# Token-major gates of the "b" heads on GpSimd, and attention units split and turned in pairs

## The chip, the cores and the metric

One core of one Trainium2 chip. The metric is the device time of one execution in microseconds (us). The engines are called PE (TensorE, matrix products), DVE (VectorE), ACT (ScalarE), POOL (GpSimd) and SP (SyncE, which here only issues DMAs).

## The reference

One encoder layer over 1024 tokens of width 1024, in float32. Two groups of attention heads run side by side; each has a gate; their gated outputs are projected, added to the input and normalised.

```python
h = x @ w_in                                   # columns: q_a k_a v_a z_a q_b k_b v_b z_b
y_a = neighborhood_attention(q_a, k_a, v_a, rel_bias)   # 8 heads of 64; grid 16 x 64,
                                                        # window 8 rows x 16 columns, 2-D bias
y_b = windowed_gqa_with_sink(rotary(q_b), rotary(k_b), v_b, sink)  # 8 query heads, 2 kv heads,
                                                        # |i - j| <= 128, one sink logit a head
mixed = concat(y_a * silu(z_a), y_b * silu(z_b))
x = layer_norm(alpha * x + mixed @ w_out, ln_gain, ln_bias)
```

## The kernel before, in words

float32 operands are kept as two float16 parts, a high and a low one, each scaled by a power of two. A product takes three matmuls: high x high, high x low, low x high.

**Stages.** First x and the weights of V are loaded and split, and V is computed. Then come 21 projections of 128 columns each, in the order of the list `ORDER`: `zb0..3` and `z0..3` are the gates of the "b" and "a" heads (two heads in each), `kb`, `qb0..3`, `k0..3`, `q0..3` the keys and queries. The first six (`NPRO`) run by themselves, in the prologue. The other 15 are "fill": their matmuls are spread among the attention's steps by a table of due steps (`FILL_AT`), so that PE always has something to do. At the end the output projection (L1031) and the normalisation follow.

**A projection** (`project`, L379) puts 128 output features on the partitions and 512 tokens in the free dimension. For each half of the tokens it runs 8 blocks of the inner dimension times 3 products, 24 matmuls, each with the weights stationary and 512 tokens moving. Gates are evacuated as SiLU (L338, or L341 and L342).

**Attention** runs over 128 units: 64 of the "b" heads (4 pairs of heads p, 2 heads j, 8 blocks of 128 queries) and then 64 of the "a" heads (p, j, 4 column bands, 2 row halves). Four units in a row are a quad. The loop over steps i emits, for several units in different stages:

- `stage_qk(u)` at step u: two score matmuls (L816, L817) into a PSUM bank of tag "s" (4 banks in turn), and one DVE instruction (L826) that adds mask or bias and takes the row maximum;
- `stage_exp(u)` at the end of step u: the exponential on ACT (L842), written back into the same PSUM bank, with the row sum;
- `stage_tr(u)` at step u+1: the high part by an ACT copy (L852), the low part by a DVE instruction (L853), both into an SBUF tile `split` (6 in turn), and a transposing DMA on SP (L856) into a tile `tr` (9 in turn);
- `stage_pv(q)` nine steps after a quad's first unit: attention times V on PE (L881) for the quad's four units;
- `stage_on(q)` one step later: DVE multiplies by the reciprocal row sums (L887, L890) into the tile `on`, with tokens on the partitions;
- `stage_ot(q)` for the second head of each pair: four PE transposes (L901) turn `on` to features on partitions, and DVE multiplies it into the gate (L904 for "b", L910 for "a").

Inside the loop the program order is kept on every engine (`manual_schedule`), and each engine runs its instructions in that order. Other work (splitting weights, evacuating projections, loading W_out) waits in a queue for each engine; `pop` takes an operation or two from a queue at fixed places of a step: for ACT after `stage_tr` (urgent ones) and after `stage_exp`, for DVE before `stage_exp`.

**The operand of the output projection** is the gated output, split in a high part (ACT, L1013) and a low part (POOL, L1014), by `m_queue` at the steps in `M_AT` for the "b" heads and in the last stage for the "a" heads.

Of the kernel before, what the change touches and what calls it, by code (L numbers as in the profile page):

```python
# [15 lines left out]
S = 1024  # L16
# [11 lines left out]
LTT, LPP, BP, BH, BR, ND, NA, NX, F1 = 1, 6, 2, 9, 5, 1, 1, 6, 0.2  # L28
NSPLIT, NP = 6, 2
ORDER = ["zb0", "z0", "zb1", "kb", "qb0", "z1", "qb1", "zb2", "qb2", "k0", "qb3", "zb3", "q0", "k1", "q1",  # L30
# [6 lines left out]
ZTAG = {"z3": "zv", "zb3": "zc", "z2": "zs", "zb1": "zd", "zb2": "ze"}  # L37
# [10 lines left out]
M_AT = [105, 112, 118, 120]  # L48
# [13 lines left out]
def hybrid_block(ctx, tc, xT, x, wt, wv, wo, bias, sink, gain, lbias, cos, sin, bmask, out):  # L62
# [9 lines left out]
    ps1 = ctx.enter_context(tc.tile_pool(name="ps1", bufs=1, space=PS))  # L72

    def bank(tag):
        bufs = {"pj": 2, "s": 4, "t": 2}[tag]
        return (ps1 if bufs == 1 else ps2).tile([128, 512], F32, tag=tag, name=f"ps_{tag}", bufs=bufs)
# [270 lines left out]
    def z_col(e):  # L347
        i = 0 if e in (4, 0, 5) else 1 if e == 1 else 2
        return zc[:, i:i + 1]
# [7 lines left out]

    def project(name):
        n = ORDER.index(name)
# [45 lines left out]
    with ExitStack() as vctx:  # L405
# [162 lines left out]
        banks = [bank(t) for t in tags]  # L568
# [49 lines left out]
        part = {i: bank(tags[i]) for i in (0, 1, 2, 3, 6, 7)}  # L618
# [138 lines left out]
    split = [ap.tile([128, 3, 2, 128], F16, name=f"split{i}", bufs=1) for i in range(NSPLIT)]  # L757
# [36 lines left out]
    def stage_qk(u):  # L794
        g, p, j, t, _ = u
        n, _c = geom(u)
        ps = bank("s")
# [31 lines left out]
        st[u, "ps"] = ps  # L829
        st[u, "nm"] = nm  # L830

    def stage_exp(u):
        n, _c = geom(u)
        m = n + 1 if u[0] == "b" else n
        sn, nm = st.pop((u, "sn")), st.pop((u, "nm"))
        pt = st.pop((u, "ps"))
        k = units.index(u) % 4
        if k == 0:
            st["sm"] = ap.tile([128, 4], F32, tag="sm", name="sm", bufs=4)
        sm = st["sm"]  # L840
        st[units.index(u) // 4, "sm"] = sm
        nc.scalar.activation(pt[:, :m], sn[:, :m], AF.Exp, bias=nm, scale=-1.0, accum_out=sm[:, k:k + 1])  # L842
        st[u, "p"] = pt

    def stage_tr(u):
        g, p, j, t, _ = u
        n, ch = geom(u)
        pt = st.pop((u, "p"))
        c, m = ch[0], len(ch)
        hl = split[units.index(u) % NSPLIT]  # L850
        src = pt[:, :n].rearrange("p (k c) -> p k c", c=c)
        nc.scalar.activation(hl[:, :m, 0, :c], src, AF.Copy, scale=PSCALE)  # L852
        nc.vector.scalar_tensor_tensor(hl[:, :m, 1, :c], src, PSCALE, hl[:, :m, 0, :c],  # L853
                                       op0=ALU.mult, op1=ALU.subtract)
        tr = ap.tile([128, 6, 128], F16, tag="tr", name="tr", bufs=BH)
        nc.sync.dma_start(tr[:, :2 * m, :], hl[:, :m].rearrange("p k i c -> p (k i c)"), transpose=True)  # L856
        st[u, "tr"] = tr
# [24 lines left out]

    def stage_on(q):
# [4 lines left out]
        if j == 0:  # L888
            on[g, p, h] = ap.tile([128, 4, 2, HD], F32, tag="on", name="on", bufs=2)
        nc.vector.tensor_mul(on[g, p, h][:, :, j, :], ps[:, :4 * HD].rearrange("p (m e) -> p m e", e=HD),  # L890
                             ri.unsqueeze(2).to_broadcast([128, 4, HD]))

    def stage_ot(q):
        g, p, j, h = quad(q)
        if j == 0:
            return
        need(*stk_ops.get(f"zb{p}" if g == "b" else f"z{p}", ()))
# [4 lines left out]
        if g == "b":  # L902
            z = zt[4 + p][:, 512 * h:512 * h + 512]
            nc.vector.scalar_tensor_tensor(z, ps, z_col(4 + p), z, op0=ALU.mult, op1=ALU.mult)  # L904
        else:
            for i in range(2):
                b = 2 * h + i
                z = zt[p].rearrange("p (r c) -> p r c", c=GW)[:, :, 16 * b:16 * b + 16]
                src = ps[:, 256 * i:256 * i + 256].rearrange("p (r c) -> p r c", c=16)
                nc.vector.scalar_tensor_tensor(z, src, z_col(p), z, op0=ALU.mult, op1=ALU.mult)  # L910
# [19 lines left out]
    def m_alloc(e):  # L930
        if e >= 4:
            t = big_tile(f"m{e}", (128, 2, S), F16)
        else:
            t = tiles["fp"].tile([128, 2, S], F16, tag="m", name=f"m{e}", bufs=4)
        mh[e], ml[e] = t[:, 0, :], t[:, 1, :]

    def m_split(e, sl, hi, lo):
        hi(mh[e][:, sl], zt[e][:, sl])
        lo(ml[e][:, sl], zt[e][:, sl], mh[e][:, sl])  # L939
# [69 lines left out]
    def m_queue(e):  # L1009
        m_alloc(e)  # L1010
        m_ops[e] = []
        for h in (slice(0, 512), slice(512, S)):
            o = enq("act", lambda h=h: nc.scalar.copy(mh[e][:, h], zt[e][:, h]))  # L1013
            m_ops[e].append(enq("pool", lambda h=h: nc.gpsimd.tensor_sub(  # L1014
                ml[e][:, h], zt[e][:, h], mh[e][:, h]), o))
# [5 lines left out]
    def out_mms(t, a, ps, es, c=(0, 512)):  # L1021
        o, w = c
        ts, cs = slice(128 * t, 128 * t + 128), slice(o, o + w)
        ps = ps[:, o:o + w]
        for e in es:
# [4 lines left out]
            for i, (lh, rh) in enumerate(((mh[e], woh), (mh[e], wol), (ml[e], woh))):  # L1030
                nc.tensor.matmul(ps, lh[:, ts], rh[:, cs],  # L1031
# [16 lines left out]
    def final():  # L1048
# [7 lines left out]
        for e in EO[4:]:  # L1056
            m_split(e, slice(0, 512), nc.scalar.copy, nc.vector.tensor_sub)
            for n in (WO_SEQ.index((e, 0)), WO_SEQ.index((e, 1))):
                wo_split(n)
        for e in EO[4:]:  # L1060
            m_split(e, slice(512, S), nc.scalar.copy, nc.vector.tensor_sub)
        gb, bb = gain_tile[0], zslot("bb")
# [113 lines left out]
    def gain_load():  # L1176
        gain_tile.append(zslot("gb"))
# [3 lines left out]
    for i in range(-LD, NU + LO):  # L1181
# [25 lines left out]
        if i == 131:  # L1207
            enq("sp", gain_load, *m_ops[4])
# [22 lines left out]
        if 0 <= i - LT < NU:  # L1231
            stage_tr(units[i - LT])
# [8 lines left out]
        pop("dve", ND if i < M_AT[1] else 2, same=True)  # L1241
        if i < NU:
            stage_exp(units[i])
        pop("act", NA if i < M_AT[0] and len(queues["act"]) < 5 else 2)
# [80 lines left out]
```

## Time and profile before

| | |
|---|---|
| median of 3 runs | 445.71 us (445.67 to 446.71) |
| the profiled execution | 446.49 us, span 444.7 us |
| busy share of the span | PE 98%, DVE 77%, ACT 69%, POOL 50% |
| granted TensorE clock, mean | 0.995 |
| attention of the "b" units | 121.8 to 237.5 us after the span's start |
| attention of the "a" units | 237.5 to 355.1 us |

In rows of the timeline the first two numbers are an instruction's start and its duration in us; then come engine, line, operation, output <- inputs, partitions x elements, and how many were merged. In rows of groups the numbers behind the bar are busy us and mean ns of one, and behind a second bar the idle us before them with what ended it. In rows of waits they are the total, the number of times, and the longest. Matmuls overlap, so their price is read from one start to the next and not from the durations.

### The profile page before, as it was taken

Reading aid. Unit: us, or ns where it says so; the run is one execution under the profiler, and the core shown is the slowest. Engines: PE = TensorE matmul, PEld = TensorE weight load, DVE = VectorE, ACT = ScalarE, POOL = GpSimd, SP = SyncE. Lnnn points to the kernel's source line nnn. Section 1 sums busy time; section 2 is a strip of 40 time slices with the busy share of each in tenths; the row PEclk is TensorE's granted clock in tenths of the full one; section 3 lists DMA queues with packets and bytes.
Section 4 is the critical chain, followed back from the end, with each engine's and each line's share of the span. In section 5 each row is a group of like instructions: output and inputs, shape, how many; then the busy total and the mean of one; then the engine's idle time right before and its main releaser. Section 6 shows DMA issues by size and latency. Waiting matters only on the chain.

```text
span 444.7 us, 9505 instructions
## 1 busy us (share of the span) xinstructions
PE 437.5 (98%) x3289; PEld 255.5 (57%) x3289; DVE 344.2 (77%) x849; ACT 308.3 (69%) x700; POOL 221.6 (50%) x235
## 2 busy tenths in 40 slices
PE   9999999999999999999999999999999999999994
PEld 8997754444445565655565655656555654444453
DVE  5978967438986898887988888888878837589944
ACT  5759789766499988887868887888778946302401
POOL 0110074646839558866506767765574405205740
PEclk9999999999999999999999999999999999999997
DMA  8921469984659999587978899998999998103612
GB/s 272 390 91 60 145 235 339 336 292 169 213 127 214 206 190 181 98 162 143 164 127 175 169 182 180 213 170 213 192 204 253 167 172 347 55 0 102 232 69 72
DMA packets 133841, 81.39 MB, mean 183 GB/s; under 512 B 101280, under 2 KB 113440, under 8 KB 133536
## 3 DMA queue, kind: packets, MB, share of 16 engines
q1 hardware_dynamic: 133648, 80.64, 75.4%
q8 instruction: 26, 0.43, 0.4%
q14 instruction: 23, 0.19, 0.2%
q10 hardware_dynamic: 144, 0.13, 0.1%
HBM read 50.34 MB, written 9.96 MB: 136 GB/s over the span
## 4 chain that ended last, share of the span: by engine, by line
PE 91%; DMA 3%; POOL 3%; DVE 1%; issue 1%; ACT 1%; SPq 0%; POOLq 0%; DVEq 0%; ACTq 0%
PE ps_pj L379 44%; PE ps_s L1031 9%; PE ps_s L486 6%; PE ps_t L881 6%; PE ps_pj L1031 5%; PE ps_t L1031 5%; PE ps_s L816 4%; PE ps_s L817 4%; PE ps_pj L486 3%; PE ps_t L486 3%; DMA bias<-in_bias 3%; PE ps_t L901 1%; POOL wl L205 1%; PE ps_t L412 1%; POOL ks L295 1%
## 5 line engine op out<-in xcount | busy, mean ns | idle before, releaser
L379 PE MATMUL ps_pj<-xf,wh 128*128 128x512 f16 x672 | 202.1, 379 | 0.1
L379 PE MATMUL ps_pj<-xf,wl 128*128 128x512 f16 x336 | 127.3, 379 | 0.0
L379 PEld LDWEIGHTS <-wh 128*128 128x128 f16 x672 | 63.7, 98 | 60.4 <-DVE ks L263 0.5
L842 ACT ACTIVATE ps_s<-sn,nm 128x385 f32<-128x385 f32 (+3 forms) x128 | 70.1, 548 | 25.1 <-DVE nm L826 24.6
L853 DVE SCALAR_TENSOR_TENSOR split<-ps_s,split 128x384 f16<-128x384 f32 (+2 forms) x128 | 65.7, 513 | 27.5 <-ACT split L852 25.9
L1031 PEld LDWEIGHTS <-m 128*128 128x128 f16 x432 | 40.0, 98 | 41.1 <-DVE m L939 0.2
L852 ACT ACTIVATE split<-ps_s 128x384 f16<-128x384 f32 (+2 forms) x128 | 57.8, 452 | 2.5 <-DMA tr<-split 0.2
L204 POOL TENSOR_SCALAR wr<-wr,wsc 128x512 f32<-128x512 f32 x26 | 20.6, 791 | 68.1 <-ACT wh L199 61.6
L379 PEld LDWEIGHTS <-wl 128*128 128x128 f16 x336 | 32.9, 98 | 37.4
L826 DVE CUSTOM_DVE_ANT_0 sn<-ps_s,bm,nsk 128x384 f32<-128x384 f32 (+1 forms) x64 | 40.7, 636 | 2.0 <-PE ps_s L817 1.7
L1031 PE MATMUL ps_s<-wo,m 128*128 128x512 f16 (+1 forms) x192 | 40.8, 366 | 0.0
L816 PE MATMUL ps_s<-ks,qs 128*128 128x384 f16 (+4 forms) x128 | 39.2, 306 | 0.3 <-DVE qs L263 0.3
L817 PE MATMUL ps_s<-ks,qs 128*128 128x384 f16 (+4 forms) x128 | 39.2, 306 | 0.0
L826 DVE CUSTOM_DVE_ANT_0 sn<-ps_s,bias,sg 128x264 f32<-128x264 f32 (+1 forms) x64 | 35.0, 547 | 4.5 <-issue 1.5
L881 PEld LDWEIGHTS <-tr 128*128 128x128 f16 (+1 forms) x1104 | 36.6, 98 | 2.2
L205 POOL TENSOR_TENSOR wl<-wr,wh 128x512 f16<-128x512 f32 x26 | 32.7, 1257 | 2.2
L788 POOL TENSOR_SCALAR bias<-bias,rsg 128x552 f32<-128x552 f32 (+1 forms) x24 | 19.1, 797 | 23.8 <-DMA bias<-in_bias 22.6
L295 POOL COPY ks<-ks 64x512 f16<-64x512 f16 x40 | 26.0, 661 | 7.1 <-DVE ks L263 2.8
L1086 ACT ACTIVATE sd<-mv,eps 128x1 f32<-128x1 f32 x8 | 2.4, 295 | 36.5 <-DVE mv L1084 35.2
L1031 PE MATMUL ps_pj<-wo,m 128*128 128x512 f16 (+1 forms) x144 | 26.2, 326 | 0.0
L1130 POOL TENSOR_TENSOR xr<-xr,gb 128x512 f32<-128x512 f32 x7 | 9.8, 1396 | 32.4 <-ACT xr L1127 32.4
L842 ACT ACTIVATION_READ_ACCUMULATOR ps_s<-sn,nm 128x1 f32 x128 | 24.4, 190 | 0.0
(188 smaller groups left out, 813.8 us busy)
## 6 DMA issues: line engine op xcount, KB each, us to landing
ws<-in_wt SPq DMA_DIRECT2D x15, 512.0 KB, 5.9
wr<-in_wt SPq DMA_DIRECT2D x26, 256.0 KB, 3.6
wor<-in_wo SPq DMA_DIRECT2D x22, 256.0 KB, 3.5
bias<-in_bias SPq DMA_DIRECT2D x16, 276.0 KB, 3.3
xr<-in_x SPq DMA_DIRECT2D x8, 512.0 KB, 9.6
out<-xr SPq DMA_DIRECT2D x15, 256.0 KB, 2.1
bias<-in_bias SPq DMA_DIRECT2D x8, 368.0 KB, 3.8
wvraw<-in_wv SPq DMA_DIRECT2D x9, 320.0 KB, 5.8
```

Source lines behind the costliest of these rows:

```text
L205: nc.gpsimd.tensor_sub(l, raw, h)
L295: nc.gpsimd.tensor_copy(t[o, sl], t[a, sl])
L379: nc.tensor.matmul(ps, a[:, k % 4, :], mv, start=(k == 0 and i == 0), stop=(k == KT - 1 and i == 2))
L486: nc.tensor.matmul(ps[:, :320], lh[:, ts], rh[:, cs], start=(k == ko[0] and i == 0), stop=(k == ko[-1] and i == 2))
L816: nc.tensor.matmul(ps[:, :m], q, sl[0], start=True, stop=False)
L817: nc.tensor.matmul(ps[:, :m], q, sl[1], start=False, stop=True)
L826: nc.vector.tensor_tensor_reduce(sn[:, :m], ps[:, :m], bias_t, sg[:, c:c + 1], init, op0=ALU.add, op1=ALU.min, accum_out=nm)
L842: nc.scalar.activation(pt[:, :m], sn[:, :m], AF.Exp, bias=nm, scale=-1.0, accum_out=sm[:, k:k + 1])
L852: nc.scalar.activation(hl[:, :m, 0, :c], src, AF.Copy, scale=PSCALE)
L853: nc.vector.scalar_tensor_tensor(hl[:, :m, 1, :c], src, PSCALE, hl[:, :m, 0, :c], op0=ALU.mult, op1=ALU.subtract)
L881: nc.tensor.matmul(ps[:, HD * m:HD * m + HD], a, b_, start=(i == 0), stop=(i == len(mms) - 1))
L1031: nc.tensor.matmul(ps, lh[:, ts], rh[:, cs], start=(e == EO[0] and i == 0), stop=(e == EO[-1] and i == 2))
```

## The change

1. **Gates of the "b" heads by tokens.** The `zb` projections get a routine of their own, `project_rows`, with the tokens on the partitions: x is stationary, 128 tokens at a time, and 128 weight columns are moving. A half is 4 token blocks x 8 x 3 = 96 matmuls of 128 columns into the same bank. All four `zb` are now in the prologue; `z0` and `z1` take the places of `zb2` and `zb3` in the fill.
2. **The product with the gate.** `stage_on` of a "b" quad scales while it normalises and queues a GpSimd multiplication of `on` into the gate (16 of 128x256 in all). `stage_ot` does nothing for "b".
3. **Turning the product.** `m_queue` splits the gated output as before (ACT, POOL) into a tile `hr`, and two transposing DMAs a head pair then write the parts, features on the partitions, over the gate's own tile. `M_AT` moves these steps from 105..120 to 26..80.
4. **Attention units in pairs.** PSUM tag "s" is now two tiles of two banks. Units 2k and 2k+1 share one. `stage_tr` runs every second step, at step 2k+2, with one ACT copy, one DVE instruction and one transposing DMA for both units (two copies and two DVE instructions where the sizes differ, as in the first and the last pair of eight "b" units). There are 3 `split` tiles and 4 `tr` tiles of twice the size.
5. Gain and bias of the normalisation get tiles of the large pool instead of gate slots.

```diff
-ORDER = ["zb0", "z0", "zb1", "kb", "qb0", "z1", "qb1", "zb2", "qb2", "k0", "qb3", "zb3", "q0", "k1", "q1",
+ORDER = ["zb0", "zb1", "zb2", "kb", "qb0", "zb3", "qb1", "z0", "qb2", "k0", "qb3", "z1", "q0", "k1", "q1",
-M_AT = [105, 112, 118, 120]
+M_AT = [26, 42, 57, 80]
...
+    def pair_bank():
+        return ps2.tile([128, 2, 512], F32, tag="s", name="ps_s", bufs=2)
...
+    def project_rows(name):
+        n = ORDER.index(name)
+        w_split(2 * n + 2)
+        for half in range(2):
+            ps = new_group()
+            need(w_ops[2 * n], w_ops[2 * n + 1])
+            for c in range(96):
+                t, k, i = c // 24, c // 3 % 8, c % 3
...
+                ts = slice(128 * t, 128 * t + 128)
+                h, l = parts[2 * n + k // 4]
+                a, b = ((x16h, h), (x16l, h), (x16h, l))[i]
+                nc.tensor.matmul(ps[:, ts], a[half, k][:, ts], b[:, k % 4, :], start=(c % 24 == 0), stop=(c % 24 == 23))
+                if c % 4 == 3 and c < 95:
+                    yield
+            groups.append(evac(name, half, ps))
+            yield
...
     def stage_qk(u):
-        ps = bank("s")
+        if units.index(u) % 2 == 0:
+            halves_s.clear()
+            st["pair"] = pair_bank()
+        ps = st["pair"][:, units.index(u) % 2, :]
...
+    def stage_tr(k):
+        pt = st.pop((k, "pair"))
+        two = [units[2 * k], units[2 * k + 1]]
+        hl = split[k % NSPLIT]
+        tr = ap.tile([128, 12, 128], F16, tag="tr", name="tr", bufs=BH)
...
+        for src, dst, f in parts_:
+            h, l = (dst[:, :, :, 0, :], dst[:, :, :, 1, :]) if f is not None else (dst[:, :, 0, :], dst[:, :, 1, :])
+            nc.scalar.activation(h, src, AF.Copy, scale=PSCALE)
+            nc.vector.scalar_tensor_tensor(l, src, PSCALE, h, op0=ALU.mult, op1=ALU.subtract)
+        w = 2 * (len(sizes[0][1]) + len(sizes[1][1]))
+        nc.sync.dma_start(tr[:, :w, :], hl.rearrange("p k i c -> p (k i c)")[:, :128 * w], transpose=True)
...
     def stage_on(q):
+        nc.vector.scalar_tensor_tensor(o, src, z_col(4 + p), rb, op0=ALU.mult, op1=ALU.mult)
+        z = zt[4 + p].rearrange("p (t j e) -> p t j e", j=2, e=HD)[:, 4 * h:4 * h + 4, j, :]
+        gate_ops.setdefault(4 + p, []).append(enq("pool", lambda: nc.gpsimd.tensor_mul(z, z, o), prio=0.6))
...
     def m_queue(e):
+            o = enq("act", lambda hr=hr, z=z: nc.scalar.copy(hr[:, :, 0, :], z), *gate_ops[e])
+            o = enq("pool", lambda hr=hr, z=z: nc.gpsimd.tensor_sub(hr[:, :, 1, :], z, hr[:, :, 0, :]), o)
+            m_ops[e].append(enq("sp", lambda hr=hr, out16=out16: nc.sync.dma_start(
+                out16, hr.rearrange("p t i f -> p (t i f)"), transpose=True), o))
...
-        if 0 <= i - LT < NU:
-            stage_tr(units[i - LT])
+        if 0 <= i - LT < NU and (i - LT) % 2 == 1:
+            stage_tr((i - LT) // 2)
```

131 lines of the change are left out of this document (77 added, 54 removed).

## The prediction

> **What bounds the kernel now.** I read the page first: the span, the busy shares, and the chain of work that ended last.
>
> ```profile
> span 444.7 us, 9505 instructions
> PE 437.5 (98%) x3289; PEld 255.5 (57%) x3289; DVE 344.2 (77%) x849; ACT 308.3 (69%) x700; POOL 221.6 (50%) x235
> PE 91%; DMA 3%; POOL 3%; DVE 1%; issue 1%; ACT 1%; SPq 0%; POOLq 0%; DVEq 0%; ACTq 0%
> ```
>
> TensorE (PE) is busy 98% and is 91% of the chain. "Busy" alone proves little, so next I read PE's own waits:
>
> ```profile
> PE ps_t L1111 <- ACT dr L1109: 1.8, 1, 1.8
> PE ps_t L412 <- DVE warm L127: 1.0, 1, 1.0
> PE ps_s L816 <- DVE qs L263: 0.3, 1, 0.3
> ```
>
> That is all: 3.1 us, and only 0.3 us of it between the first projection and the tail. So PE is never held up, and two things move the time: PE work added or taken away, at full price, and anything that makes PE wait where today it waits for nobody. The profiled execution took 446.49 us around a span of 444.7; that is 0.78 above the median of 445.71. I add the sum to the profiled one and take the 0.78 off at the end.
>
> **PE's own work.** The prices come from starts in the timeline, because matmul durations overlap:
>
> ```profile
> 157.17 0.60 PE L901 MATMUL ps_t<-identf,on 128*128 128x128 f32 x4
> 157.61 1.13 PE L881 MATMUL ps_t<-vb,tr 128*128 128x64 f16 x33
> 158.57 0.60 PE L379 MATMUL ps_pj<-xf,wh 128*128 128x512 f16 x2
> 159.00 0.38 PE L379 MATMUL ps_pj<-xf,wl 128*128 128x512 f16 x1
> 159.22 0.59 PE L379 MATMUL ps_pj<-xf,wh 128*128 128x512 f16 x2
> ...
> 434.08 2.84 PE L1031 MATMUL ps_pj<-wo,m 128*128 128x128 f16 x48
> 436.76 0.65 PE L1104 MATMUL ps_t<-bb,identf 128*128 128x256 f32 x2
> ```
>
> Three 512-column matmuls go in 159.22 - 158.57 = 0.65 us, 216.7 ns each. Forty-eight 128-column ones, each with its own weight load, go in 2.68 us: 55.8 ns each. The four "zb" projections have 4 x 2 x 24 = 192 of the first kind (41.6 us); by tokens they become 4 x 2 x 96 = 768 of the second (42.9 us): **+1.3 us**. Could the four times as many weight loads show? The 33 attention-times-V matmuls load new weights every 0.96/33 = 29 ns, so a load hides behind 55.8 ns.
>
> The transposes of the "b" heads go: eight times four, and four take 157.61 - 157.17 = 0.44 us, so **-3.5 us**.
>
> The first projection now asks for both halves of its weights almost at once:
>
> ```profile
> 59.27 1.16 POOL L205 TENSOR_TENSOR wl<-wr,wh 128x512 f16<-128x512 f32 x1
> 59.37 0.59 PE L379 MATMUL ps_pj<-xf,wh 128*128 128x512 f16 x2
> ```
>
> It starts at 59.37. In token order the second half's low part is needed after 14 matmuls, 14 x 0.056 = 0.8 us later, at 60.15; GpSimd finishes it at 60.43: **+0.3 us**. In the old order it was needed 14 x 0.217 = 3 us in, and hidden. PE's own sum is -1.9 us. If nothing else happened, the time would be 443.8.
>
> **What the pairs do to PSUM.** Today each unit has one of four banks, and bank i is needed again by unit i+4, three steps after the step that empties it. After the change the banks come as two pairs. A pair is emptied by one ScalarE copy (high part) and one VectorE subtraction (low part) in the step of unit 2k+2; the scores of unit 2k+4, two steps later, need it back. PE takes its instructions in order, so when that wait is not met everything behind it stands: fill matmuls, scores, attention times V.
>
> Does it matter? Look at how the two engines hand the work to each other, one quad (two pairs) of the "b" heads; of the rows between, those of the even units are left out:
>
> ```profile
> 152.18 0.67 DVE L826 CUSTOM_DVE_ANT_0 sn<-ps_s,bm,nsk 128x384 f32<-128x384 f32 x1
> ...
> 153.12 0.59 ACT L842 ACTIVATE ps_s<-sn,nm 128x385 f32<-128x385 f32 x1
> 153.72 0.72 ACT L199 ACTIVATE wh<-wr,wsc 128x512 f16<-128x512 f32 x1
> 154.33 0.48 ACT L852 ACTIVATE split<-ps_s 128x384 f16<-128x384 f32 x1
> 154.85 0.56 DVE L853 SCALAR_TENSOR_TENSOR split<-ps_s,split 128x384 f16<-128x384 f32 x1 [0.30 <-ACT split L852]
> 155.32 0.17 DVE L887 RECIPROCAL ri<-sm 128x4 f32<-128x4 f32 x1
> 155.52 0.42 DVE L890 TENSOR_TENSOR on<-ps_t,ri 128x256 f32<-128x256 f32 x1
> 155.87 0.67 DVE L826 CUSTOM_DVE_ANT_0 sn<-ps_s,bm,nsk 128x384 f32<-128x384 f32 x1
> 156.58 0.59 ACT L842 ACTIVATE ps_s<-sn,nm 128x385 f32<-128x385 f32 x1 [0.18 <-DVE nm L826]
> 157.19 0.71 ACT L199 ACTIVATE wh<-wr,wsc 128x512 f16<-128x512 f32 x1
> 157.81 0.47 ACT L852 ACTIVATE split<-ps_s 128x384 f16<-128x384 f32 x1
> 158.31 0.56 DVE L853 SCALAR_TENSOR_TENSOR split<-ps_s,split 128x384 f16<-128x384 f32 x1
> 158.78 0.67 DVE L826 CUSTOM_DVE_ANT_0 sn<-ps_s,bm,nsk 128x384 f32<-128x384 f32 x1
> ```
>
> This is the loop of the odd units: bias and maximum (L826), exponential (L842), whatever ScalarE has queued (L199 here), copy (L852), subtraction (L853), whatever VectorE has queued (L887, L890), and only then the L826 of the unit two further. Both engines run in program order, so it is a true loop. It took 158.78 - 152.18 = 6.60 us for two pairs, of which 0.23 is ScalarE coming late at 153.12 (0.94 us after L826 started, against 0.71 at 155.87 to 156.58). Bare: 6.37.
>
> In the changed order the same instructions stand in this loop, but the copy and the subtraction now carry both units, while the even unit's share has left the place where it ran beside the loop. What 384 more columns cost comes from the small and the large form (the large ones are in the fence above: 0.48 and 0.56):
>
> ```profile
> L852 ACT ACTIVATE split<-ps_s 128x256 f16<-128x256 f32 x15 | 5.7, 381 | 0.4
> L853 DVE SCALAR_TENSOR_TENSOR split<-ps_s,split 128x256 f16<-128x256 f32 x15 | 6.3, 422 | 2.6 <-ACT split L852 2.4
> ```
>
> ScalarE: (480 - 381)/128 = 0.77 ns a column, +0.30 us; VectorE: (560 - 422)/128 = 1.08 ns, +0.41. So +0.71 a pair, and this quad's loop becomes 6.37 + 1.42 = 7.8 us. PE's pace:
>
> ```profile
> L816 PE MATMUL ps_s<-ks,qs x64: 269/326/326, 121.8 to 236.2; 128*128 128x384 f16 x48, 128*128 128x256 f16 x16
> L816 PE MATMUL ps_s<-ks,qs x64: 276/304/326, 237.5 to 355.1; 128*128 128x264 f16 x16, 128*128 128x288 f16 x16, 128*128 128x352 f16 x16, 128*128 128x384 f16 x16
> ```
>
> "b": (237.5 - 121.8)/32 = 3.62 us a pair, less 3.5/32 for the transposes, 3.51. "a": (355.1 - 237.5)/31.5 = 3.73. Two "b" pairs are 7.0 us of PE against 7.8 of the loop: the saving in instructions on ScalarE and VectorE is real, but the loop gets longer, and overtakes PE.
>
> To see whether that quad is typical I added up the same pieces (without VectorE's waits for PE) at 31 odd "b" units and 30 odd "a" units; the first and last of each:
>
> ```profile
> 127.24 0.67 DVE L826 CUSTOM_DVE_ANT_0 sn<-ps_s,bm,nsk 128x384 f32<-128x384 f32 x1
> 239.21 0.53 DVE L826 CUSTOM_DVE_ANT_0 sn<-ps_s,bm,nsk 128x256 f32<-128x256 f32 x1
> 242.74 0.51 DVE L826 CUSTOM_DVE_ANT_0 sn<-ps_s,bias,sg 128x288 f32<-128x288 f32 x1
> 350.68 0.61 DVE L826 CUSTOM_DVE_ANT_0 sn<-ps_s,bias,sg 128x384 f32<-128x384 f32 x1
> ```
>
> "b": 3.35 us a pair now. Half the pairs join units of unequal size (the first two and last two blocks); these keep two copies and two subtractions, which overlap, and add only 0.4 to 0.5, so the mean becomes 3.96. "a": 3.23 now, sizes 288 and 384 in turn, becomes 3.86. The excess over PE is 0.45 x 32 = 14.4 us in "b" and 0.13 x 32 = 4.2 in "a". Single pairs run from 2.5 to 6.7 us, so how much is paid depends on PE's lead: a running sum over the 61 pairs gives 16 us with a lead of 2 us and 24 with 1 us. The lead is about 3 x 1.8 steps less the bare loop's 3.5, some 1.8. I take **+18 us**.
>
> **What else moves.** Groups of instructions, the time from issue to landing of the transposes, and one stretch of the tail:
>
> ```profile
> L904 DVE SCALAR_TENSOR_TENSOR z<-ps_t,zc,z 128x512 f32<-128x512 f32 x8 | 6.0, 747 | 0.0
> L1099 POOL TENSOR_TENSOR xr<-xr,gb 128x256 f32<-128x256 f32 x1 | 0.7, 728 | 0.2 <-DVE stats L1080 0.2
> DMA to landing us min/median/max: 2.5/3.4/6.2
> 440.00:442.00 2.00, 0.69 (x2) 0.00 (x0) 0.56 (x1) 0.37 (x1) 0.00 (x0) 0.50 0.23 71
> ```
>
> L904 leaves VectorE (8 x 0.75 = 6 us), but it ran in odd steps, outside the loop: no gain. Its product becomes 16 GpSimd multiplications of 256 columns, 16 x 0.73 = 12 us on an engine at 50%: off the path, because the first reader of the gated "b" heads is the output projection after step 121, some 50 steps later; without that cover it would be those 12 us. The eight 512-column copies of L1013 move forward out of the late "a" units; one that lands between exponential and copy lengthens the loop as L199 does above (153.72 to 154.33), by 0.6, so 0 to 5 us together; I take 0, because half the slots are beside the loop and the queue gives one copy a step, and keep 5 for the range. Scaling inside L890 is one more scalar in the same pass: 0. On SP, 64 larger transposing DMAs replace 128, and eight more are queued; whoever is behind them on SP waits at most for their issue, and attention times V comes five steps after the last transpose. Gain and bias of the norm load earlier, which removes waits in the tail that PE does not feel: 0.
>
> **Sum.** 446.49 + 1.3 + 0.3 - 3.5 + 18 = 462.6 in a profiled execution; less 0.78, **461.8 us**. Its own range: 453 if ScalarE's queued work shifts to the even slots (0.15 less a pair in "b") and "a" stays hidden; 472 with a lead of 1 us and the L1013 copies in the loop.
>
> **Rivals.** (1) *The loop does not bind* (chance 0.20, faster): PE's lead covers it, because the 6 us of L904 and the shorter totals let VectorE catch up, or the halves of a pair come free separately. The point is a loop mean under 3.51. For it: the loop today, 3.35, never stops PE; against it, today's loop leaves so little that +0.4 is enough. Time: 443.8. (2) *The doubled transposes land late* (0.05, slower): the median is 3.4, the slowest 6.2. A pair's transpose has about three steps, 5.5 us, before PE reads it once PE waits for banks; twice the data at twice 3.4 would miss by 1.3 us in 32 quads, some of it inside waits already there: about 475. (3) *The clock drops* (0.03): the last row in the fence above is no term of the sum but shows the granted clock (its third number from the end): 0.50 in two us near the end, in which PE has little to do. If the waits gather in a few pairs, such as those with a loop of 6.7 us, PE pauses 3 us and may come back at half speed; doubling the 3.5 us of PE work of three such pairs adds 10 us: 472. Against it: the mean wait is 0.3 us a pair. [...] (4) *The gains and waits cancel* (0.03): within 0.3% of before, which is about what a measurement of this kernel can tell.
>
> **Chances and range.** The forecast has 0.69; with rivals 2 and 3, slower is 0.77; same 0.03; faster 0.20. As both signs count, the range reaches from rival 1 to the forecast's upper end: 443.5 to 473; the forecast's own is 453 to 472.
>
> **What would show it.** In the profile after: PE's waits list L816 behind VectorE's subtraction or "split" with 10 to 25 us in all, PE busy falls to about 94%, the score matmuls of "b" take 3.9 to 4.0 us a pair instead of 3.62. The prologue is 1.6 us longer, the final projection unchanged, and the L853 of equal pairs take 0.95 us. If PE's waits stay under 2 us, the loop argument is wrong and rival 1 holds; if they name the transposes at L881, rival 2.

## The result, and the profile after

The changed kernel takes **513.96 us** (median of 6 runs, 511.74 to 514.91) against 445.91 for the kernel before (445.67 to 446.71) on the same chip: a ratio of 1.152, 95% interval 1.1495 to 1.1545. The forecast was 461.8 with a range to 473. The sign was right; the size was wrong by 52 us.

The page of the changed kernel, first the busy shares and the chain, then PE in 40 slices:

```profile
span 512.5 us, 10275 instructions
PE 448.9 (88%) x3833; PEld 277.4 (54%) x3833; DVE 340.7 (66%) x793; ACT 306.0 (60%) x652; POOL 233.0 (45%) x248
PE   9999999998767878886877789899997979999995
PE 21%; issue 7%; ACT 6%; DVE 6%; DMA 3%; POOL 3%; SPq 1%; POOLq 0%; DVEq 0%; ACTq 0%
```

PE falls from 98% to 88% busy, and the holes lie in the slices of attention (122.9 to 422.6 us) and in the last slice, which was as empty before. No other engine has become the bound: VectorE and ScalarE were 77% and 69% busy and are now 66% and 60%. Everybody waits for somebody.

PE's score matmuls, and what ended the idle time in front of them (total us, number of times); below that, who else waits most:

```profile
L856 PE MATMUL ps_s<-ks,qs x128: 269/322/406, 122.9 to 422.6; 128*128 128x384 f16 x64, 128*128 128x256 f16 x16, 128*128 128x264 f16 x16, 128*128 128x288 f16 x16
  ACT ps_s L883: 40.9, 45
  DVE sn L861: 7.5, 5
  DVE split L907: 3.3, 3
```

```profile
ACT ps_s L883 <- DVE nm L866: 74.4, 71, 3.8
```

The forecast had PE waiting for the subtraction (L907 now, L853 before): the profile puts 3.3 us down to it. What PE waits for is the **exponential** (L883, 40.9 us), which in the kernel before held up no score matmul at all. All of the 53.5 us idle in front of the scores stands before scores of *odd* units, none before even ones. The stops that the profile puts down to another engine are the same stop: the odd scores start 0.04 to 0.06 us after the last row of the even unit's exponential there too, as here, where it ends at 208.50 + 0.19 = 208.69 us and a subtraction happens to end with it:

```profile
208.50 0.19 ACT L883 ACTIVATION_READ_ACCUMULATOR ps_s<-sn,nm 128x1 f32 x1
208.74 0.32 PE L856 MATMUL ps_s<-ks,qs 128*128 128x384 f16 x1 [0.94 <-DVE split L907]
```

So nearly the whole 53.5 us is the exponential's.

One pair in the timeline of the changed kernel (start, duration, engine, line; in brackets the idle time before and what ended it). Rows of other lines are left out:

```profile
152.42 0.57 ACT L883 ACTIVATE ps_s<-sn,nm 128x385 f32<-128x385 f32 x1
152.92 0.18 ACT L883 ACTIVATION_READ_ACCUMULATOR ps_s<-sn,nm 128x1 f32 x1
...
153.16 0.32 PE L856 MATMUL ps_s<-ks,qs 128*128 128x384 f16 x1 [1.66 <-ACT ps_s L883]
153.79 0.68 DVE L866 CUSTOM_DVE_ANT_0 sn<-ps_s,bm,nsk 128x384 f32<-128x384 f32 x1 [0.30 <-ACT z L350]
...
154.51 0.59 ACT L883 ACTIVATE ps_s<-sn,nm 128x385 f32<-128x385 f32 x1 [0.83 <-DVE nm L866]
155.03 0.19 ACT L883 ACTIVATION_READ_ACCUMULATOR ps_s<-sn,nm 128x1 f32 x1
156.93 0.62 ACT L268 CAST qs<-rp_raw 64x512 f16<-64x512 f32 x1 [1.71 <-POOL rp_raw L324]
157.46 0.80 ACT L906 ACTIVATE split<-ps_s 128x768 f16<-128x768 f32 x1
158.16 0.57 ACT L883 ACTIVATE ps_s<-sn,nm 128x385 f32<-128x385 f32 x1
...
158.90 0.27 PE L856 MATMUL ps_s<-ks,qs 128*128 128x256 f16 x1 [1.60 <-ACT ps_s L883]
```

Read it as a ring. The even unit's exponential ends at 153.10, and 0.06 us later the odd unit's scores start, after 1.66 us of idle PE. The two touch different banks: the exponential writes columns 0 to 384 of the pair's tile, the scores write from column 512 on. Nothing in the arithmetic asks for this order, but the program has it: both halves are now one tile, and the odd unit's first score matmul waits until the exponential in that tile is done. (That the joint tile is the reason is an inference here; the runs below test it.) So the ring closes: even exponential (152.42) to odd scores (153.16), to the odd bias and maximum (153.79), to the odd exponential (154.51, until 155.22), to the copy of this pair (0.70 us, 157.46 to 158.16), and to the even exponential of the next pair, which stands behind it in ScalarE's order. Without the gap from 155.22 to 157.46 that is 0.74 + 0.63 + 0.72 + 0.71 + 0.70 = 3.50 us a pair, and PE itself needs 3.51 (as the prediction worked out). That leaves no slack; whatever else ScalarE has in its queue between the odd exponential and the copy goes on top. Here that is a cast which itself waited 1.71 us for GpSimd, and the pair took 158.16 - 152.42 = 5.74 us.

### The profile page after: what moved, and what is told of

Read it like the earlier page. It is cut to its first block, busy times and chain, and to the rows that moved or that the text cites. A ratio compares the mean times of both kernels' runs of the same rounds, so it can differ in the third digit from the quotient of the medians.

```text
span 512.5 us, 10275 instructions
## 1 busy us (share of the span) xinstructions
PE 448.9 (88%) x3833; PEld 277.4 (54%) x3833; DVE 340.7 (66%) x793; ACT 306.0 (60%) x652; POOL 233.0 (45%) x248
## 5 line engine op out<-in xcount | busy, mean ns | idle before, releaser
L416 PE MATMUL ps_pj<-xf,wh 128*128 128x512 f16 x544 | 165.7, 383 | 0.0
L883 ACT ACTIVATE ps_s<-sn,nm 128x385 f32<-128x385 f32 (+3 forms) x128 | 70.2, 548 | 75.0 <-DVE nm L866 74.4
L416 PE MATMUL ps_pj<-xf,wl 128*128 128x512 f16 x272 | 103.9, 382 | 0.0
L856 PE MATMUL ps_s<-ks,qs 128*128 128x384 f16 (+4 forms) x128 | 39.1, 306 | 53.5 <-ACT ps_s L883 40.9
L907 DVE SCALAR_TENSOR_TENSOR split<-ps_s,split 128x768 f16<-128x768 f32 (+3 forms) x80 | 58.4, 729 | 33.4 <-ACT split L906 32.5
L866 DVE CUSTOM_DVE_ANT_0 sn<-ps_s,bm,nsk 128x384 f32<-128x384 f32 (+1 forms) x64 | 41.0, 641 | 34.7 <-PE ps_s L857 28.3
L906 ACT ACTIVATE split<-ps_s 128x768 f16<-128x768 f32 (+3 forms) x80 | 49.8, 622 | 16.4 <-DVE split L907 15.4
L866 DVE CUSTOM_DVE_ANT_0 sn<-ps_s,bias,sg 128x264 f32<-128x264 f32 (+1 forms) x64 | 35.2, 551 | 33.6 <-issue 14.7
L857 PEld LDWEIGHTS <-qs 128*128 128x128 f16 x128 | 12.4, 97 | 75.4 <-issue 67.7
L386 PEld LDWEIGHTS <-xf 128*128 128x128 f16 x768 | 43.2, 98 | 0.6 <-issue 0.3
L386 PE MATMUL ps_pj<-wh,xf 128*128 128x128 f16 x512 | 43.4, 219 | 0.0
L386 PE MATMUL ps_pj<-wl,xf 128*128 128x128 f16 x256 | 43.2, 219 | 0.2 <-POOL wl L214 0.2
L1097 PEld LDWEIGHTS <-m 128*128 128x128 f16 x216 | 20.3, 98 | 21.4 <-DVE m L999 0.2
L1097 PEld LDWEIGHTS <-z 128*128 128x128 f16 x216 | 19.9, 98 | 19.7
```

What stands on the lines that cost most here:

```text
L386: nc.tensor.matmul(ps[:, ts], a[half, k][:, ts], b[:, k % 4, :], start=(c % 24 == 0), stop=(c % 24 == 23))
L416: nc.tensor.matmul(ps, a[:, k % 4, :], mv, start=(k == 0 and i == 0), stop=(k == KT - 1 and i == 2))
L856: nc.tensor.matmul(ps[:, :m], q, sl[0], start=True, stop=False)
L857: nc.tensor.matmul(ps[:, :m], q, sl[1], start=False, stop=True)
L866: nc.vector.tensor_tensor_reduce(sn[:, :m], ps[:, :m], bias_t, sg[:, c:c + 1], init, op0=ALU.add, op1=ALU.min, accum_out=nm)
L906: nc.scalar.activation(h, src, AF.Copy, scale=PSCALE)
```

## The experiments

The kernels came in five groups, each with runs of the kernel before on the same chip; those stood between 446.18 and 447.06 us. Ratios are to them, with 95% intervals.

### The two halves of the change apart

**Gates alone**: the change with four one-bank score tiles and with copy, subtraction and transfer by unit, as before.

> The change without its pairs: token-major gates, GpSimd product and transposed parts stay; PSUM, split and tr are by unit as before. Theory W (the odd unit's scores wait for the even unit's exponential because both lie in one PSUM tile): nothing of the loss is left, PE's own sum decides, 443.8 us (443 to 445). Theory L (the loop of copy and subtraction, as predicted): the same 443.8. Theory G (the gates cost the time through GpSimd, SP or the tighter start): 450 or more.

Measured 459.28 us, ratio 1.0295 (1.0279 to 1.0312): theory G's number. The gates lose time of their own.

**Pairs alone**: the kernel before with item 4 of the change.

> Only the pairs, put into the kernel before. Theory W: the whole loss and a little more, since the gates' PE gain of 1.9 us is missing: 513 to 520 us, PE idle before odd scores 50 us or more, none before even scores. Theory L alone: 460 to 466. Theory G: under 450.

Measured 509.87 us, ratio 1.141 (1.136 to 1.146): 3 us under theory W's range, with its signs, 50.6 us of idle PE before odd scores and none before even ones. So the pairs bring most of the loss: +63.7 us without the gates, and 513.96 - 459.28 = 54.7 on top of them.

### The tile, the late emptying, the late release

**Pair tiles only**: the kernel before, each unit still copied, subtracted and sent by itself; only the allocation differs.

```diff
+    def pair_bank():
+        return ps2.tile([128, 2, 512], F32, tag="s", name="ps_s", bufs=2)
...
-        ps = bank("s")
+        if units.index(u) % 2 == 0:
+            halves_s.clear()
+            st["pair"] = pair_bank()
+        ps = st["pair"][:, units.index(u) % 2, :]
```

> The kernel before with one edit: PSUM tag s is two tiles of two banks instead of four of one; copies, subtractions and transposes stay by unit and at their old steps. Theory W: odd scores wait for the even exponential here too, but the copies ahead of it are short, so 460 to 500 us with all of PE's waits before odd scores. Theory L: the loop is not longer, 445 to 448.

Measured 522.56 us, ratio 1.1723 (1.1693 to 1.1752): as large a loss as any here, with no wide instruction and no pairwise transfer in it. It is 22 us over theory W's range: the place of the waits was right, their size was not. What ended the idle time before its scores (L853 is the exponential in this kernel), again before odd ones only:

```profile
L827 PE MATMUL ps_s<-ks,qs x128: 269/322/521, 121.9 to 430.3; 128*128 128x384 f16 x64, 128*128 128x256 f16 x16, 128*128 128x264 f16 x16, 128*128 128x288 f16 x16
  ACT ps_s L853: 60.8, 61
```

**Four one-bank tiles**: the changed kernel, all of it by pairs as changed, but with a tile for each bank, and so two copies and two subtractions for every pair.

> The change with four PSUM tiles of one bank again; the two units of a pair are still split in one step (two copies, then two subtractions) and turned by one DMA. Theory W: the wait of the odd scores is gone and with it at least 50 of the 68 us. If the predicted loop L then binds: 455 to 468 us, PE waiting before even scores for the subtraction. If W is all there is: 444 to 446.

Measured 464.9 us, ratio 1.0426 (1.0407 to 1.0444). The wait for the exponential is gone, and 49 of the 68 us with it (theory W had at least 50). The 8.1 us behind the subtraction now stand before even scores, as theory L had it. PE's waits there (us in total, times, longest):

```profile
PE ps_s L845 <- DVE split L889: 8.1, 8, 3.0
PE ps_t L1013 <- DVE wom L1004: 3.5, 1, 3.5
PE ps_t L1159 <- ACT dr L1157: 1.8, 1, 1.8
PE ps_s L845 <- DVE qs L264: 1.1, 1, 1.1
```

**Emptying put off**: the kernel before, single banks, with `stage_tr` of both units of a pair in the step of unit 2k+2.

```diff
-        if 0 <= i - LT < NU:
+        if 0 <= i - LT < NU and (i - LT) % 2 == 1:
+            stage_tr(units[i - LT - 1])
             stage_tr(units[i - LT])
```

> The kernel before with one edit: both units of a pair are split, by two copies and two subtractions with two transposes, in the step of unit 2k+2; four PSUM tiles of one bank. This is the predicted loop by itself. Theory L with the predicted size: 458 to 464 us. If the loop is worth only the difference of single_banks and gates_only, 5.6 us: 450 to 453. If PE's lead hides it: 446.

Measured 454.69 us, ratio 1.0183 (1.0164 to 1.0202), between the expected ranges, with 4.3 us of PE waits for the subtraction, all before even scores. This is the loop that the prediction was built on, in the form with two copies and two subtractions, and it is worth +8.2 us by itself, or 464.9 - 459.28 = 5.6 beside the gates.

Next, two attempts to take the order away without giving up the wide tiles. **Late exponential**: in the changed kernel the even unit's exponential is issued after the odd scores.

```diff
-        if i < NU:
+        if i < NU and i % 2 == 1:
+            stage_exp(units[i - 1])
             stage_exp(units[i])
```

> The changed kernel with one move: the exponential of an even unit is issued after the odd unit's scores and bias step instead of before them; tiles, copies, subtractions and transfers stay in pairs over two banks. Theory W (the 49 us between the changed kernel and four one-bank tiles are the odd scores' wait for the even exponential, which exists only since both halves are one tile): no PE wait on the exponential is left, and 461 to 470 us. Rival V (the wide copies and subtractions over two banks, or banks that come free late, are what costs): over 495 us, the wait merely moves to the subtraction or to the bias step.

Measured 522.23 us, ratio 1.1674 (1.1646 to 1.1703): theory W's number failed. **The same with a third buffer** for the biased scores:

> The changed kernel with the even exponential issued after the odd scores, as before, and a third buffer for the biased scores, so that the bias steps need not wait for the exponentials (which the run without it showed: 85 us of ScalarE's waits for the bias step and of VectorE's for ScalarE). Of the one-tile order only the even unit's bias step is left ahead of the odd scores, and it ends about 0.8 us after the even scores, well inside the 1.75 us that PE spends on a unit. Theory W (the loss is that the halves of one tile are put in order, and it shrinks with the event that the odd scores must wait for): 465 to 485 us. Rival V (the wide copies and subtractions, or banks that come free late, are what costs): over 495 us, with PE waiting for the subtraction.

Measured 522.64 us, ratio 1.1692 (1.1674 to 1.1711). A miss again, and the number that rival V had given. The waits of this last kernel:

```profile
PE ps_s L856 <- DVE nm L866: 28.8, 34, 2.4
PE ps_s L856 <- DVE split L907: 22.2, 29, 2.1
```

```profile
DVE split L907 <- ACT split L906: 98.5, 74, 2.8
```

The odd scores now wait for the bias step of the even half, L866 (28.8 us), and the even scores for the subtraction (22.2 us). I had taken the bias step as harmless because it ends 0.8 us after the scores; but it stands in VectorE's queue behind a subtraction, which stands behind ScalarE's copy, which now stands behind two exponentials (98.5 us of VectorE's waits). With the tile in one piece, another arrangement closed another ring. These two runs leave open whether the order of the halves or the joint release of both banks makes the rings expensive. That was settled by the **joint release without the order**: the kernel of four one-bank tiles, odd unit copied and subtracted first (both loops), so that the even bank, which is needed first, comes free last.

```diff
-        for h, l, src in todo:
+        for h, l, src in reversed(todo):
```

> The kernel of four one-bank tiles (464.9 us), with the two copies and the two subtractions of a pair in the opposite order, odd unit first. The even unit's bank now comes free only with the last subtraction of the pair, as it does in the changed kernel, but nothing puts the odd scores behind the even exponential. Theory W (the order between the halves is what costs 49 us, the joint release next to nothing): 463 to 472 us, with the waits before the scores behind the subtraction, under 15 us. Rival V (the late release of both banks at once is what costs): over 490 us, with more than 30 us of PE waits for the subtraction.

Measured 464.74 us, ratio 1.0405 (1.0376 to 1.0433), as without it. PE's wait for the subtraction:

```profile
PE ps_s L845 <- DVE split L889: 9.7, 13, 3.1
```

In single banks, late release costs nothing that can be measured here. With that rival gone, the order between the halves of one tile is left as what costs the 49 us. (The wide copies and subtractions were not run without the wide tile; the kernel with pair tiles only has the loss without them.)

### What the gates cost

The gates alone lose 13.1 us where the prediction had -1.9. PE's longest single wait in that kernel is for the scale of the output weights:

```profile
PE ps_t L1006 <- DVE wom L997: 4.8, 1, 4.8
PE ps_s L845 <- DVE split L882: 3.7, 4, 1.4
```

**Scale later**: gates alone, `WO_SCALE` 55 to 64.

> Gates only, with one number changed: the scale of W_out, which needs the maxima of all its 16 blocks, is formed at step 64 instead of 55. Theory S (the transposes of the product took the places of W_out's loads in SP's queue, so that the last maximum came late and PE waited 4.8 us and then ran at half clock for some us): about 8 of the 13 us go, 451 us (449 to 453). Theory A (ACT's copies and DVE's lateness cost the time, not SP): 457 to 459.

Measured 455.35 us, ratio 1.0199 (1.0178 to 1.022): between theory S (449 to 453) and theory A (457 to 459). The wait was worth 4 us, half of what S had.

**Parts later**: gates alone, `M_AT` at 96, 100, 104 and 108 instead of 26 to 80.

> Gates only, with M_AT at 96, 100, 104, 108: ACT copy, GpSimd subtraction and transpose of the gated parts come after W_out's loads. Theory S or A, both of which blame these early steps: nothing but PE's own sum is left, 443 to 446 us. Theory P (the token-major projections or the GpSimd products themselves cost it): 455 or more.

Measured 464.84 us, ratio 1.0416 (1.0396 to 1.0436): worse, and theory P's number. The "a" units take 131.4 us from the first score of "a" to the last score, against 117.5 with the early parts, and the loss lies in the steps from 104 to 116, just behind those at which the late parts are queued. **The same on the four one-bank tiles**:

> The change with four PSUM tiles of one bank (as in single_banks) and with M_AT at 96, 100, 104, 108. If the two causes add, it loses the 13 us of the early parts and keeps the 5.6 of the pairs: 449 to 452 us. If the pairs' loop only cost time because ACT was full of early copies: 444 to 446.

Measured 469.4 us, ratio 1.0508 (1.048 to 1.0536): both expectations missed. So the early place is the better one; but it isn't free, which the next runs take apart.

**Without the turns**: gates alone, scale at 55, without the 8 transposing DMAs (the edit's other place, the operand of the output projection, is left out here).

```diff
-            m_ops[e].append(enq("sp", lambda hr=hr, out16=out16: nc.sync.dma_start(
-                out16, hr.rearrange("p t i f -> p (t i f)"), transpose=True), o))
+            m_ops[e].append(o)
```

> The gates alone with the output weights' scale left at step 55 (459.3 us), without the 8 transposing DMAs of the product's parts; the output projection takes its moving operand's partner for the 'b' parts from the weights instead. Theory S (SP's queue hands out one transfer a step, so the 8 turns put the last loads of the output weights back, and the scale at step 55 makes PE wait 4.8 us): the wait before ps_t L1006 falls under 1 us and the time to 454 to 456 us, as with the scale moved to step 64 (455.4). Rival T (the late maximum has another cause, VectorE's queue): the wait stays over 3 us and the time over 458.

Measured 453.88 us, ratio 1.0156 (1.0134 to 1.0179), a little better than S had it. The scale's wait is gone. The last maximum that the scale needs, in the timeline of the gates alone and then of this kernel:

```profile
231.78 0.69 DVE L997 TENSOR_REDUCE wom<-wor 128x1 f32<-128x512 f32 x1
```

```profile
224.79 0.68 DVE L997 TENSOR_REDUCE wom<-wor 128x1 f32<-128x512 f32 x1
```

The maximum before it comes at the same time in both, within 0.14 us (219.29 and 219.15). The program lets SP's queue hand out one transfer a step, and the turns took the places of the last weight loads: in the gates alone two turns go out at 215.21 and 220.30 us and the last load of the output weights at 224.86; without turns it goes out at 218.71. The four waits for late attention transposes (1.5 us in the gates alone) went too.

**Without the products**: gates alone, scale at 64, without the 16 GpSimd multiplications.

> The gates alone with the output weights' scale at step 64 (455.4 us in the earlier run), and now without the 16 GpSimd products of 0.73 us: the 'b' gate tiles keep the gate alone, and the product's parts are made of the scaled gate. That run lost about 7 us of PE time in attention at a few places, all of which stood behind a ScalarE queue that waited for a late GpSimd step (2.6 us for the rotary sum, 2.0 us for another rotary product). Theory P (the added products make GpSimd's rotary steps late, and ScalarE, then VectorE's subtraction, then PE wait in turn): the stalls of 1.3 and 1.75 us go, 455.4 -> 449 to 452 us, and ScalarE's waits for rp_raw fall from 6 us to under 3.5. Rival Q (the products are hidden as the prediction had it; SP's turns or the changed order of the projections make the rest): within 1 us of 455.4.

Measured 452.24 us, ratio 1.012 (1.0096 to 1.0145), against 1.0199 with them: about 3.5 us. Theory P's signs hold, with a time just above its range of 449 to 452. PE's waits for the subtraction fall from 4.5 us to 0.2. In the kernel with the products, ScalarE had waited for GpSimd like this:

```profile
ACT qs L260 <- POOL rp_raw L316: 4.0, 4, 2.6
ACT z L342 <- POOL rp_raw L314: 2.0, 1, 2.0
```

Without them, 2.6 us of the 6.0 are left, as P had it (under 3.5):

```profile
ACT z L342 <- POOL rp_raw L314: 2.3, 1, 2.3
ACT qs L260 <- POOL rp_raw L316: 0.3, 1, 0.3
```

GpSimd is 43 to 52% busy in all these kernels, yet a rotary step that leaves it 2.6 us late blocks ScalarE's queue, exponentials and copies behind it included.

**Products on VectorE**, nothing left out:

> The same kernel with the 16 products on VectorE instead of GpSimd, from VectorE's own queue, with nothing left out. 16 products of an estimated 0.35 us (a quarter of a million elements less than the 0.48 us step that makes on) go to an engine that is 66% busy. Theory P: GpSimd is on time again, 450 to 453 us. Rival Q: 455 to 457 us, since VectorE only gets more to do. Rival R (VectorE is the tighter engine in the stretch of 'b' units): over 458 us, with PE waits for the subtraction over 6 us.

Measured 462.53 us, ratio 1.034 (1.0315 to 1.0365): rival R by its time, though PE's waits behind the subtraction are 4.5 us, not over 6, and 3.7 more name GpSimd. One product takes VectorE 703 ns in the mean, twice my estimate (whose reason was wrong too: the step that makes `on` has the same 128x256 elements):

```profile
L928 DVE TENSOR_TENSOR z<-z,on 128x256 f32<-128x256 f32 x16 | 11.3, 703 | 0.3
```

The mean hides two kinds. Seven of the 16 take 0.41 to 0.42 us, and beside five of these GpSimd has no instruction at all; the other nine take 0.49 to 1.41 us, and GpSimd works beside each of them.

**Without products and turns** (scale at 55):

> The gates alone (scale at step 55) with neither the 16 GpSimd products nor the 8 turns; both are left out, the parts are made of the scaled gate, and the output projection reads weights in their place. What is left of the change is the row projections, their order, the scaling step 0.06 us longer and the 32 transposes that are gone. If the two left-out steps are all that the gates lose beside the prediction's own sum: 443.8 us by that sum with the prologue 1.9 us late, so 443 to 447 us and within 0.5 per cent of the kernel before. Rival U (the changed order of the projections costs by itself, or the losses are one lateness counted twice): 449 to 453 us, not below the run without the turns by more than 2 us.

Measured 450.18 us, ratio 1.008 (1.0059 to 1.0102): rival U's range, though it is 3.7 us below the run without the turns, where U allowed 2. So the two losses add up, and something else is left. **Without the parts as well**:

> The run without products and turns (450.2 us), and without the 8 copies and 8 subtractions that make the parts of the 'b' heads' product either (they stood at steps 105 to 120 before, and stand at 26 to 80 in the change; here they are left out). That run's last stall, 2.2 us, stood behind a ScalarE step that waited 2.3 us for GpSimd, which had one of those subtractions (1.16 us) just ahead. If the early parts are the third cause: no PE wait for the subtraction over 0.5 us, and 446.5 to 449 us. Rival (the order of the projections, which alone is left, puts the rotary products late): 449.5 to 451.5 us and the 2.2 us stall stays.

Measured 449.63 us, ratio 1.0065 (1.0038 to 1.0093): on the boundary between the two expectations, and no different from the run with the parts. One PE wait of 1.3 us for the subtraction stays, behind ScalarE's 1.8 us for a rotary step. The parts as a third cause have no support here.

So of the gates' 13.1 us: 6.3 are the turns in SP's queue (13.1 - 6.8), 3.6 the products on GpSimd (6.8 - 3.2), and 3.2 remain with the row projections and their order. (Each figure is against the kernel before on the same chip.) In the profile of the kernel without products and turns, the prologue is 1.6 us longer, as forecast, and the tail 0.8 shorter. From the first to the last score matmul it takes 235.6 us against 233.3, where 3.5 less were forecast. Most of that lies in one quad, which is 4.1 us longer than before: PE stops for 2.24 us behind the subtraction, and its clock is then at half for some 3.4 us. ScalarE had waited there for a rotary product of GpSimd:

```profile
209.69 0.69 ACT L342 ACTIVATE z<-ps_pj,invt 128x512 f32<-128x512 f32 x1 [2.28 <-POOL rp_raw L314]
212.22 0.32 PE L845 MATMUL ps_s<-ks,qs 128*128 128x384 f16 x1 [2.24 <-DVE split L882]
```

In the kernel before, ScalarE waits 1.8 us for the same step and PE does not stop. The order of the projections is what differs; it was not run by itself, so this cause stays open.

## Why the prediction was right or wrong

**The step that failed** is the description of PSUM under "What the pairs do to PSUM": a pair "is emptied by one ScalarE copy (high part) and one VectorE subtraction (low part)", and only "the scores of unit 2k+4" were taken to wait for it. I treated the two banks as independent until they were released. The program does not: odd scores wait for the even exponential in the same tile. That is 49 us (513.96 against 464.9), in no term of the sum and in none of the rivals. The text even came near it, in rival 1 ("or the halves of a pair come free separately"), but asked only about the end of a tile's life, not about the time when one half is being written while the other is read. That the sign came out right is largely luck: most of the loss comes from a wait that the prediction does not have. Without that wait the time is 464.9, close to the forecast's 461.8, but for other reasons: 13.1 us of it are the gates' (forecast -1.9) and 5.6 the loop's (forecast 18). The Trainium skill, "PSUM — Partial Sum Buffer" (PSUM bank collisions raise a hardware error), asks for guarding PSUM by bank and quadrant; by that rule the halves, which are two banks, need no order between them. The run with one-bank tiles agrees: there PE never waits for the exponential, and the time is 464.9 us.

**The loop** was the right mechanism, and its size is not settled: +18 us forecast, +5.6 (beside the gates) to +8.2 (alone) measured. The waits were where it said, behind the subtraction and before even scores, but 4.3 to 8.1 us of them. The two are not the same loop, though. The kernels measured make two copies and two subtractions for every pair, and to that form the prediction itself gave 0.4 to 0.5 us a pair, not the 0.71 of the wide one. With 0.45 for all, its own means come to 3.35 + 0.45 = 3.80 against 3.51 in "b", 9 us over 32 pairs, and to nothing in "a" (3.68 against 3.73): an estimate near the 8.2 measured. The wide form never bound: in the changed kernel no even score waits. The widths were priced rightly: the pairs of equal size take 799 and 956 ns, against 0.78 and 0.95 us worked out.

```profile
L907 DVE SCALAR_TENSOR_TENSOR split<-ps_s,split 128x768 f16<-128x768 f32 x32 | 30.6, 956 | 16.4 <-ACT split L906 15.6 <-POOL wr L213 0.6
L906 ACT ACTIVATE split<-ps_s 128x768 f16<-128x768 f32 x32 | 25.6, 799 | 0.4
```

**PE's own work** came as priced where nothing disturbed it. The wait at the first row projection was 0.2 us (forecast 0.3), and the prologue grew by 1.1 to 2.2 us in the kernels with row projections (forecast 1.6). In gates-alone kernels eight undisturbed "b" units take 14.67 us against 15.11 before; the removed transposes were to give 3.5/8 = 0.44.

```profile
PE ps_pj L386 <- POOL wl L214: 0.2, 1, 0.2
```

**The moves costed at nothing** were the second error. "Whoever is behind them on SP waits at most for their issue" looked at the time of an issue, not at the rule of one transfer a step: +6.3. The products "off the path", because their reader comes 50 steps later, looked at who waits for the product and not at who stands behind it in GpSimd's queue: +3.6. The early copies and subtractions (0 to 5, taken as 0) cost nothing measurable once turns and products were gone.

**The signs to look for**, one by one: PE's wait behind the subtraction 3.3 us by the profile, and even these end with the exponential (forecast 10 to 25); PE busy 88% (94); "b" pairs (280.7 - 122.9)/32 = 4.93 us (3.9 to 4.0; the "a" units begin at 280.7); the first scores 1.1 us later (1.6). The last score matmul to the end of the span takes 89.9 us against 89.6, the final projection unchanged, as forecast. Rival 2 (late transposes) did not come: 1.2 us of PE waits name them, and that stop too ends with the exponential. Rival 3 (the clock) did, in part: three stretches of some 3.4 us at half clock, about 5 us lost, where it had 10. It doubled 3.5 us of work each time, but a stretch of 3.4 us at half clock holds only 1.7 us of work.

**The sum of the loss.** The first to the last score matmul take 299.7 us against 233.3, 66.4 more. Idle before scores is 53.5 of it, and the wait for the scale 2.4. In the same stretch PE is busy 243.9 us against 232.9, although it has 3.5 us less to do:

```profile
122.90:280.70 157.80, 121.49 (x968) 64.01 (x966) 98.54 (x260) 100.15 (x239) 87.41 (x91) 0.98 0.66 128
280.70:422.60 141.90, 122.39 (x1089) 68.60 (x1088) 94.43 (x234) 91.97 (x210) 70.20 (x88) 0.99 0.86 166
```

The lower clock (0.98 and 0.99 against 1.00) explains 158 x 0.02 + 142 x 0.01, about 4.6 us. The rest, some 9 us, would be about 0.17 us for each of some 55 restarts; that is a division, not a measurement.

No kernel of these beats the one before.

## What to carry to other kernels

Before two buffers are joined into one tile, list every write and read of each half in program order and ask which of them the tile will now put in sequence; a wait between halves that share no data does not show in the arithmetic, and it can close a ring between engines that were a pipeline. Price a ring by its bare sum against the pace of the bound engine (3.50 against 3.51 us here), then add whatever else those engines have queued. And when work moves to a queue that is "half idle", ask not who waits for its result but who stands behind it in that queue.

## What the runs showed of the hardware

PE's clock fell three times within the attention of the changed kernel, from about 202.5, 243.4 and 284.4 us on, each time to half for some 3.4 us. Each fall came 0.1 to 0.7 us after the end of a listed gap of idle PE, of 2.23, 2.36 and 2.10 us. After the gap of 2.36 us (until 243.31), these windows of 2 us show the granted clock as the third number from the end:

```profile
242.00:244.00 2.00, 0.69 (x5) 0.42 (x5) 1.43 (x4) 1.57 (x5) 1.09 (x2) 0.85 0.51 99
244.00:246.00 2.00, 2.00 (x35) 1.74 (x33) 1.28 (x3) 1.72 (x4) 1.13 (x1) 0.50 1.30 110
246.00:248.00 2.00, 2.00 (x9) 0.89 (x8) 0.00 (x0) 0.48 (x2) 1.54 (x2) 0.79 0.52 109
```

The length of the gap alone does not decide: another of 2.40 us, before the scale of the output weights at 261.00, left the clock at 1.00. In the tail of the kernel before, the clock fell to 0.50 (from 440 us on) behind a listed gap of 1.81 us. The Trainium skill, "TensorE: Matmul & The Clock Gate" (Part 1), gives an idle window of about 3.4 us for the fall; here listed gaps of 1.81 to 2.36 us were enough, and one of 2.40 was not.

A 128x256 multiplication in float32, with all operands in runs of 64 elements, took 727 ns on GpSimd (median of 16 in the changed kernel, 722 to 735). On VectorE it took 415 to 1407 ns, with a mean of 703: about 0.42 us where GpSimd was idle beside it, and up to 1.4 where GpSimd worked throughout. The move to VectorE saved nothing in the mean. That GpSimd's work is what stretches the long ones is seen only as a coincidence in time; no run here tests it.
